# Rows for the convolution's layer norm and for later token rates: sent through DRAM in place of PE transposes

## The chip, the cores and the metric

The kernel runs on one core of a Trainium2 chip. The metric is the device time of one execution in microseconds, of which three were measured: 1282.7, 1285.05 and 1284.26 us, with a median of 1284.26 us. A profile of one further execution shows what each engine did: PE (matrix products and transposes, with its weight loads listed as PEld), DVE, ACT and POOL (element-wise work), and SP, which issues most of the transfers.

## The reference

One layer of a hybrid encoder runs over 2048 tokens of 1024 channels, with 16 learned tokens ahead of them. A projection feeds two groups: a gated depthwise convolution with a layer norm over channels, and a stick-breaking attention with 8 heads of 64 channels. Both are concatenated, projected again, normalised and added to the input.

```
u = rms_norm(h, pre_g)
proj = u @ w_in                      # 3584 columns: glu_a, glu_b, conv_gate, q, k, v, sb_gate
c = glu_a * sigmoid(glu_b)
c = causal_depthwise_conv(c, conv_w, conv_b)          # width 31
c = silu(layer_norm(c, conv_ln_g, conv_ln_b))         # mean and variance over 512 channels
c = (c @ w_pw2 + b_pw2) * silu(conv_gate)
s = stick_breaking_attention(q, k, v) * silu(sb_gate)
return h + rms_norm(concat([c, s]) @ w_out, post_g)
```

## The kernel before

Tokens are worked in four chunks of 512 (`TC`), c = 0 to 3. Activations lie turned: channels on the 128 partitions, tokens along the free axis, so a quantity that belongs to a token (a mean, a rate) has to stand as a row of 512 numbers that is the same on all partitions. Every float32 product is made of three passes with split high and low parts, and PE carries all of them.

A Python-side scheduler writes the program. It keeps a model clock (`Clock`, `Engine`), runs three streams of pieces against each other in `merge` (attention as `main`, projections, norm and output products as `fill`, and `extra`), and emits work noted with `when` as soon as the model says that its inputs are there. A piece that PE takes waits until the model has its inputs ready for `slack` (1.0 us). Any operation added or removed therefore shifts the order of everything emitted after it. Each engine then executes its own list strictly in order, and SP too: a transfer whose wait is not met holds all transfers behind it.

The part around the change is `conv_norm(c, accs)`. When the four convolution sums `accs[j]` of a chunk (128 channels x 512 tokens each) are there, PE turns them in four blocks of 128 tokens into a PSUM bank `T` (of which there are four), and DVE takes mean and variance per token (`bn_stats`, `bn_aggr`), which gives a column of 128 numbers. `rstd_of` makes the rate on POOL. Then the columns are made into rows twice, first the means and then the rates: four PE transposes of a broadcast column against the identity fill one bank `T`, and DVE applies the row to the four sums (`apply`, subtraction for i = 0, product with the gain for i = 1). `swish` follows, then `conv_parts` splits the result and `conv_out` multiplies it, much later in the program.

`spread_later(c)` does the same for the norm ahead of the input projection of chunks 1 to 3: four transposes of a column of `later` give the row of token rates, which ACT copies to the tile `row` for c > 1, and DVE multiplies it into the input tiles `xs` (`times_rate`, `scale`).

The lines that make a row of means or rates before:

```
rows[i] = PT("T", [P, TC])
for tb in range(NTB):
    pe.transpose(
        rows[i][:, tb * P : (tb + 1) * P], cols[tb].to_broadcast([P, P]), ident
    )
for j in range(NJ):
    when(
        lambda j=j, i=i: apply(j, i), [rows[i], accs[j]], [accs[j]]
    )
```

Of the kernel before, what the change touches and what calls it, by code (L numbers as in the profile page):

```python
# [11 lines left out]
F32 = mybir.dt.float32  # L12
F32R = mybir.dt.float32r
BF16 = mybir.dt.bfloat16
AF = mybir.ActivationFunctionType
ALU = mybir.AluOpType
# [3 lines left out]
P = 128  # L20
# [3 lines left out]
NM = 16  # L24
TC = 512
NCH = SEQ // TC
NTB = TC // P
CC = 512
NJ = CC // P
# [15 lines left out]
LAGS, LEAD = 1.5, 0.2  # L45
TAP, APART_TAP = 0.67, 1.25
EARLY = 6
LAG = 3

WINDOW = 10.0  # L50
# [226 lines left out]
def trunk(ctx: ExitStack, tc: tile.TileContext, x, xturn, xlater, meta, cpack, post_g, wpack, out):  # L277
    nc = tc.nc
# [15 lines left out]
    def when(what, ins, outs=(), engine=None, date=0.0, tag=None, late=0.0):  # L294
        soon.append(Later(clock, what, ins, outs, engine, date, tag, late))

    pe = Engine(clock, nc.tensor, pe_cost, 0.15, run)
    dve = Engine(clock, nc.vector, dve_cost, 0.04, run)
    act = Engine(clock, nc.scalar, act_cost, 0.04, run)
    pool = Engine(clock, nc.gpsimd, pool_cost, 0.04, run)  # L300
    sp = Engine(clock, nc.sync, sp_cost, 0.0, run)
# [9 lines left out]
    dr = ctx.enter_context(tc.tile_pool(name="dr", bufs=1, space=DRAM))  # L311
# [14 lines left out]
    def T(tag, shape, bufs, dt=F32):  # L326
        room(tag, bufs)
        t = sb.tile(shape, dt, tag=tag, name=tag, bufs=bufs)
        clock.take(tag, bufs, t.name)
        return t  # L330

    def PT(tag, shape):
        bufs = BANKS[tag]
        room(tag, bufs)
        t = ps.tile(shape, F32, tag=tag, name=tag, bufs=bufs)
        clock.take(tag, bufs, t.name)
        return t
# [3 lines left out]
    def need(*aps, tag=None, given=None, evs=0, n=1):  # L341

        def at():
            if given and not given():
                return 1e6
            t = max([clock.at(a) for a in aps] + [0.0])
            if tag:
                t = max(t, clock.next_free(tag, n))  # L350
            if evs:

                t = max(t, clock.next_free("ev", evs) - 1.0)
            return t + slack[0]

        return at


    ident = const.tile([P, P], F32, name="ident")
# [8 lines left out]
    lng = cp[:, o + NJ : o + 2 * NJ]  # L368
# [16 lines left out]
    row = const.tile([P, NM + TC], F32, name="row")  # L385
# [24 lines left out]
    vscr = dr.tile([NJ, NM + SEQ, 2 * P], F32, name="vscr")  # L410
    sscr = dr.tile([NCH, NJ, P, TC], F32, name="sscr")
    gscr = dr.tile([NCH, NJ, P, TC], F32, name="gscr")

    u_now = []
    xs = {}
# [20 lines left out]
    def tap_apart():  # L436
        tap(taps_apart)
# [11 lines left out]
    def rstd_of(acc, n, eps, rows=P, cols=1):  # L449
        v = T("st1", [P, cols], 4)  # L450
        pool.tensor_scalar(v[:rows], acc[:rows], 1.0 / n, eps, op0=ALU.mult, op1=ALU.add)
        r = T("st2", [P, cols], 8)
        pool.tensor_tensor(
            r[:rows], v[:rows], nhalf[:rows].to_broadcast([rows, cols]), op=ALU.pow
        )
        return r
# [93 lines left out]
    for turn, (w, n0, cols, ka, kb) in specs():  # L550
        step_k = 4 * P // cols
        for k0 in range(ka, kb, step_k):
            key = w, n0, cols, k0
            n = (min(k0 + step_k, kb) - k0) * cols
# [257 lines left out]
        renewed(c)  # L812

    def spread_later(c):
        pt = PT("av" if c == 1 else "T", [P, TC])
        for tb in range(NTB):
            n = (c - 1) * NTB + tb
            pe.transpose(
                pt[:, tb * P : (tb + 1) * P], later[:, n : n + 1].to_broadcast([P, P]), ident
            )  # L820
        keep["row", c] = pt
        if c > 1:
            act.activation(row[:, NM:], pt, AF.Copy)
            keep["row", c] = row[:, NM:]
        for k in range(KD):
            if (c, k) in xs:
                times_rate(c, k)

    later = T("sq2", [P, 4 * NTB], 1)
# [224 lines left out]
    def meta_v(h):  # L1054
        e, j = h % 2, h // 2
        force(f"v{j}")
        for g in range(3):
# [4 lines left out]
            )  # L1062
        if h >= EARLY:
            sp.dma_start(
# [17 lines left out]
    keep = {("z", -1): True}  # L1082
# [17 lines left out]
    def conv_apart(c, j):  # L1100
# [15 lines left out]
            pool.tensor_tensor(acc, acc, this, op=ALU.add)  # L1116
        accs[c][j] = acc

    def conv_norm(c, accs):
        def summed():  # L1120
            if len(accs) == NJ:
                return pe.now
            return max(dve.now, pool.now, pe.now) + 2.0 if taps or taps_apart else 1e6

        yield summed
        while taps:
            tap()
        while taps_apart:
            tap_apart()


        rows = {}
        rates = [None] * NTB

        def rate(tb, mv):
            rates[tb] = rstd_of(mv[:, 1:2], 1, 1e-5)

        means = []
        for tb in range(NTB):
            yield need(*(accs[j][:, tb * P : (tb + 1) * P] for j in range(NJ)), tag="T")  # L1140
            pt = PT("T", [P, CC])
            for j in range(NJ):
                pe.transpose(
                    pt[:, j * P : (j + 1) * P], accs[j][:, tb * P : (tb + 1) * P], ident
                )
            st = T("bst", [P, 6], 3)
            dve.bn_stats(st, pt)
            mv = T("bmv", [P, 2], 5)
            dve.bn_aggr(mv, st)
            means.append(mv)  # L1150
            when(lambda tb=tb, mv=mv: rate(tb, mv), [mv])
        done = []

        def apply(j, i):
            if i:
                dve.scalar_tensor_tensor(
                    accs[j], accs[j], lng[:, j : j + 1], rows[i], op0=ALU.mult, op1=ALU.mult
                )
            else:
                dve.tensor_tensor(accs[j], accs[j], rows[i], op=ALU.subtract)  # L1160
            done.append((j, i))

        for i in range(2):
            if i:
                yield need(given=lambda: None not in rates and len(done) == NJ)
            cols = rates if i else [mv[:, 0:1] for mv in means]
            yield need(*cols, tag="T")
            rows[i] = PT("T", [P, TC])
            for tb in range(NTB):
                pe.transpose(  # L1170
                    rows[i][:, tb * P : (tb + 1) * P], cols[tb].to_broadcast([P, P]), ident
                )
            for j in range(NJ):
                when(
                    lambda j=j, i=i: apply(j, i), [rows[i], accs[j]], [accs[j]]
                )
        yield need(given=lambda: len(done) == 2 * NJ)
        def swish(j):
            b, y, sg = lnb[:, j : j + 1], accs[j], PT("T", [P, TC])
            act.activation(sg, y, AF.Sigmoid, bias=b)  # L1180
            when(
                lambda: dve.scalar_tensor_tensor(y, y, b, sg, op0=ALU.add, op1=ALU.mult),
                [y, sg], [y],
            )

        for j in range(NJ):
            when(
                lambda j=j: swish(j), [accs[j]], [accs[j]], date=pe.now + 1.5 * j, tag="T"
            )
        keep["normed", c] = True  # L1190
# [73 lines left out]
    def attention(c, mixs):  # L1264
# [41 lines left out]
        def scan(r, u, zs, zr):  # L1306
# [18 lines left out]
            prev[r] = u["a"][r] = pr  # L1325
            if kc == 0 and c == NCH - 1 and h >= EARLY:
                bm = keep["bm"][:, h - EARLY, r, h]
                zm = sgm[:, r, h, 0:NM]
# [611 lines left out]
    accs = [{} for _ in range(NCH)]  # L1940
# [141 lines left out]
```

## Time and profile before

| what | value |
|---|---|
| median of three runs | 1284.26 us |
| the profiled execution's own time | 1282.96 us |
| its span, first to last instruction | 1281.2 us |
| busy PE / DVE / ACT / POOL | 1270.7 / 1009.5 / 790.0 / 681.0 us |
| granted PE clock | 0.999 |
| HBM traffic | 218.95 MB read, 66.98 MB written |

Busy time is the time in which an engine had at least one instruction under way. A matmul's duration runs from its start to a modelled end, and several overlap, so what one takes of PE's time is read from the distance between starts. "Idle before" is the time an engine stood still ahead of a group, with the engine or transfer whose signal ended it. The 1.76 us between span and time lie outside the first and last instruction.

### The profile page before, as it was taken

The page shows a single profiled execution, that of the slowest core. Times are in us where ns is not written, and L with a number is a line of the kernel's source. Part 1 is how long each engine was busy: PE and PEld are TensorE (multiplying, and loading weights), DVE is VectorE, ACT ScalarE, POOL GpSimd, SP SyncE. Part 2 cuts the span into 40 slices and gives each one's busy share as a digit, 9 for nine tenths or more (in the row PEclk, how much of TensorE's full clock was granted, in tenths as well). Part 3 has the DMA queues.
Part 4 walks back from the last instruction along what each step waited for, and adds up shares of the span by engine and source line. Part 5 has one row for each costly group of instructions (what it writes and reads, how often), then busy time and mean ns, then how long its engine had stood idle before and what let it go on. Part 6 is the DMA issues. An engine that isn't in the chain of part 4 may idle for free.

```text
span 1281.2 us, 22398 instructions
## 1 busy us (share of the span) xinstructions
PE 1270.7 (99%) x7463; PEld 1104.3 (86%) x7463; DVE 1009.5 (79%) x1434; ACT 790.0 (62%) x1696; POOL 681.0 (53%) x805
## 2 busy tenths in 40 slices
PE   9999999999999999999999999999999999999997
PEld 8998888888899888888889988888888899888897
DVE  5999998898987488984567587985548888899974
ACT  6544456445456464777655546789877766656553
POOL 2555569867687430677872231388788522232402
PEclk9999999999999999999999999999999999999999
DMA  6688876687988885676966695657668555576745
GB/s 245 214 275 266 268 252 220 208 262 244 288 274 270 292 294 178 209 234 211 295 198 212 178 339 176 179 180 230 201 223 256 150 152 185 169 250 216 222 150 183
DMA packets 175876, 289.79 MB, mean 226 GB/s; under 512 B 21120, under 2 KB 72512, under 8 KB 175760
## 3 DMA queue, kind: packets, MB, share of 16 engines
q1 hardware_dynamic: 164528, 250.87, 63.0%
q0 software_dynamic: 11232, 37.49, 7.8%
q8 instruction: 59, 0.97, 0.3%
q14 instruction: 57, 0.47, 0.1%
HBM read 218.95 MB, written 66.98 MB: 223 GB/s over the span
## 4 chain that ended last, share of the span: by engine, by line
PE 95%; DMA 2%; DVE 1%; POOL 1%; issue 0%; ACT 0%; SPq 0%; DVEq 0%; POOLq 0%; ACTq 0%
PE mm L228 63%; PE T L228 22%; PE av L228 10%; DMA tok<-x 1%; DMA wr<-wpack 0%; DVE ul L228 0%; PE cv L228 0%; DMA wr<-wscr 0%; DMA pr<-xturn 0%; DVE tok L228 0%; POOL st L228 0%; ACT ev L228 0%; DVE bst L228 0%; DVE T L228 0%; SPq L228 0%
## 5 line engine op out<-in xcount | busy, mean ns | idle before, releaser
L228 PE MATMUL mm<-uh,w 128*128 128x512 f32 (+1 forms) x1936 | 562.3, 376 | 0.0
L228 PEld LDWEIGHTS mm<-uh,w 128*128 128x128 f32 x1936 | 336.6, 188 | 50.9 <-ACT uh L228 0.3
L228 PE MATMUL mm<-ul,w 128*128 128x512 f32 (+1 forms) x968 | 358.2, 371 | 0.1
L228 DVE TENSOR_TENSOR_SCAN pr<-T,pr,zcol 128x512 f32<-128x512 f32 (+1 forms) x224 | 268.6, 1200 | 47.7 <-ACT T L228 37.7
L228 DVE TENSOR_TENSOR al<-T,ah 128x512 fp32r<-128x512 f32 (+1 forms) x320 | 191.6, 600 | 97.3 <-ACT ah L228 95.2
L228 DVE SCALAR_TENSOR_TENSOR cv<-ct,cp,cv 128x512 f32<-128x512 f32 x319 | 239.1, 750 | 6.8
L228 ACT ACTIVATE ah<-T 128x512 fp32r<-128x512 f32 (+1 forms) x320 | 169.3, 530 | 108.5 <-PE T L228 106.1
L228 POOL TENSOR_TENSOR acc<-acc,pd 128x512 f32<-128x512 f32 x150 | 193.6, 1290 | 59.3 <-ACT pd L228 52.1
L228 PEld LDWEIGHTS mm<-ul,w 128*128 128x128 f32 x968 | 181.3, 188 | 33.8 <-DVE ul L228 0.5
L228 POOL TENSOR_TENSOR w<-wr,w 128x512 fp32r<-128x512 f32 x130 | 169.9, 1309 | 66.8 <-ACT w L228 58.6
L228 ACT ACTIVATE T<-T 128x512 f32<-128x512 f32 (+5 forms) x352 | 169.7, 489 | 51.4 <-PE T L228 45.7
L228 ACT ACTIVATE w<-wr 128x512 fp32r<-128x512 f32 x220 | 137.9, 628 | 85.2 <-PE mm L228 45.1
L228 PE MATMUL T<-kk,q 128*128 128x512 f32 (+4 forms) x704 | 190.4, 365 | 0.0
L228 PE MATMUL T<-ident,pr 128*128 128x128 f32 x1088 | 171.1, 272 | 0.0
L228 PEld LDWEIGHTS T<-ident,pr 128*128 128x128 f32 x1088 | 134.2, 140 | 29.3 <-DVE al L228 0.2
L228 PEld LDWEIGHTS T<-kk,q 128*128 128x128 f32 x704 | 113.4, 189 | 14.4 <-DVE pr L228 0.7
L228 PE MATMUL av<-ah,vk 128*128 128x512 f32 (+1 forms) x320 | 117.7, 368 | 0.0
L228 PE MATMUL av<-al,vk 128*128 128x512 f32 (+1 forms) x320 | 116.9, 365 | 0.0
L228 DVE TENSOR_TENSOR_SCAN pr<-T,tri 128x128 f32<-128x128 f32 (+3 forms) x128 | 87.6, 688 | 33.0 <-ACT T L228 30.6
L228 ACT ACTIVATE pd<-ct,cp 128x512 f32<-128x512 f32 x150 | 105.6, 715 | 0.9 <-POOL acc L228 0.8
L228 POOL COPY cm<-pr 128x1 f32<-128x1 f32 x120 | 24.3, 203 | 124.3 <-DVE pr L228 117.9
L228 POOL TENSOR_TENSOR ev<-ev 64x512 f32<-64x512 f32 (+2 forms) x46 | 55.6, 1208 | 56.6 <-ACT ev L228 38.3
(202 smaller groups left out, 1570.7 us busy)
## 6 DMA issues: line engine op xcount, KB each, us to landing
wr<-wpack SPq DMA_DIRECT2D x220, 256.0 KB, 3.9
w<-wscr SPq DMA_DIRECT2D x70, 512.0 KB, 4.6
vk<-vscr SPq DMA_DIRECT2D x80, 256.0 KB, 3.5
w<-lscr SPq DMA_DIRECT2D x80, 256.0 KB, 2.7
kk<-kscr SPq DMA_DIRECT2D x72, 256.0 KB, 4.2
q<-qscr SPq DMA_DIRECT2D x64, 256.0 KB, 5.4
wscr<-w POOLq DMA_DIRECT2D x28, 512.0 KB, 4.8
lscr<-w POOLq DMA_DIRECT2D x40, 256.0 KB, 3.8
```

The lines of the kernel that those rows point to most:

```text
L228: return call(out, *args, **kw)
```

## The change

For chunks 1 to 3, the means and rates of the convolution norm no longer pass PE. A transfer on SP writes the column of 128 x 4 numbers to a small DRAM tile `nscr` as 512 consecutive numbers (`spread_out`), and a second one reads them back to all 128 partitions as a tile `nrow` in SBUF, 128 x 512 (`load`). It is noted for 6 us (`SPREAD`) after the first. There is one `nrow` buffer, so the rates' load waits until the means have been subtracted. Chunk 0 keeps its PE transposes. Token rates of chunks 2 and 3 go the same way, straight into `row`. The four mean and variance columns now lie in one tile `bmv`, and `rstd_of` runs once over four columns rather than four times over one. The room set aside for POOL's transfer descriptors is halved.

```
+    nscr = dr.tile([NCH, 3, 1, TC], F32, name="nscr")
...
     def spread_later(c):
+        if c > 1:
+            n = (c - 1) * NTB
+            date = spread_out(c, 2, later[:, n : n + NTB]) + SPREAD
+            when(lambda: row_later(c), [], date=date)
+            return
...
+    def row_later(c):
+        keep["row", c] = row[:, NM:]
+        sp.dma_start(row[:, NM:], nscr[c, 2].to_broadcast([P, TC]))
+        times_rates(c)
...
+    def spread_out(c, i, col):
+
+        sp.dma_start(nscr[c, i, 0].rearrange("(t p) -> p t", p=P), col)
+        return pe.now
...
+        mvs = T("bmv", [P, NTB, 2], 2)
+        sent, done = {}, []
+
+        def send(i, col):
+            sent[i] = spread_out(c, i, col) if c else col
+
+        def load(i):
+            t = T("nrow", [P, TC], 1)
+            sp.dma_start(t, nscr[c, i].to_broadcast([P, TC]))
+            put_in(i, t)
...
+        when(lambda: send(0, mvs[:, :, 0]), [mvs])
+        when(lambda: later_on(rstd_of(mvs[:, :, 1], 1, 1e-5, cols=NTB)), [mvs])
...
+        for i in range(2):
+            yield need(given=lambda: i in sent and len(done) == i * NJ)
+            if c:
+                when(lambda i=i: load(i), [], date=max(pe.now, sent[i] + SPREAD))
             else:
...
-    nc = _bacc.Bacc("TRN2", target_bir_lowering=False, num_devices=1, dynamic_dma_scratch_size=4096)
+    nc = _bacc.Bacc("TRN2", target_bir_lowering=False, num_devices=1, dynamic_dma_scratch_size=2048)
```

On PE, behind the turn of chunk 1's convolution sums, these rows stood before (`T<-ident,bmv` makes the row of means, `T<-ident,st` that of rates, `mm` rows are output products, `av` and `T<-kk` attention):

```order
L228 MATMUL av<-al,vk 128x512
L228 MATMUL T<-ident,bmv 128x128 x4
L228 MATMUL T<-ident,pr 128x128 x2
L228 MATMUL mm<-w,mixs 128x256 x12
L228 MATMUL T<-kk,q_4270 128x272 x2
L228 MATMUL av<-ah,vk 128x512
L228 MATMUL av<-al,vk 128x512
L228 MATMUL T<-ident,st_4677 128x128
L228 MATMUL T<-ident,st_4701 128x128
L228 MATMUL T<-ident,st_4720 128x128
L228 MATMUL T<-ident,st_4724 128x128
L228 MATMUL mm<-w,mixs 128x256 x12
```

The same place on PE now:

```order
L229 MATMUL av<-al,vk 128x512
L229 MATMUL mm<-w,mixs 128x256 x12
L229 MATMUL T<-ident,pr 128x128 x2
L229 MATMUL T<-kk,q_4256 128x272 x2
L229 MATMUL mm<-w,mixs 128x256 x12
L229 MATMUL av<-ah,vk 128x512
L229 MATMUL av<-al,vk 128x512
L229 MATMUL mm<-w,mixc 128x256 x12
```

Eight transposes are gone here, the rest stands in a slightly other order; in all PE has 7431 matmuls instead of 7463, with 12 fewer on `bmv`, 12 fewer on `st` and 8 fewer on the token rates `sq`, and no other kind changed in number.

On DVE, behind chunk 1's `BN_AGGR` (the mean and variance), this stood before; `acc<-acc,T` subtracts the means and `acc<-acc,cp,T` multiplies by rates and gain, while `al` and `pr` are attention:

```order
L228 SCALAR_TENSOR_TENSOR pr<-T,pr,zcol 128x512
L228 TENSOR_TENSOR acc<-acc,T 128x512 x4
L228 TENSOR_TENSOR al<-T,ah 128x256
L228 SCALAR_TENSOR_TENSOR pr<-T,tri 128x256
L228 SCALAR_TENSOR_TENSOR acc<-acc,cp,T 128x512 x4
L228 TENSOR_TENSOR al<-T,ah 128x128
```

DVE's list now, from the sixth row behind that `pr` on:

```order
L229 SCALAR_TENSOR_TENSOR pr<-T,tri 128x264
L229 SCALAR_TENSOR_TENSOR pr<-T,pr,zcol 128x248
L229 TENSOR_TENSOR acc<-acc,nrow 128x512 x4
L229 TENSOR_TENSOR al<-T,ah 128x512
L229 SCALAR_TENSOR_TENSOR pr<-T,tri 128x128
L229 SCALAR_TENSOR_TENSOR pr<-T,pr,zcol 128x512
L229 TENSOR_TENSOR al<-T,ah 128x512
L229 SCALAR_TENSOR_TENSOR acc<-acc,cp,nrow 128x512 x4
L229 TENSOR_TENSOR al<-T,ah 128x512
```

The subtraction stands seven attention rows further back than it did, and the product with the rates four rows behind the subtraction; both now read `nrow`.

On SP, the new transfers of chunk 1 stand so, between loads of weights (`wr`), keys, values and queries (`kk`, `vk`, `q`):

```order
L229 DMA nscr<-bmv 128x4x1
L229 DMA wr<-wpack 128x512 x2
L229 DMA nscr<-st_4696 128x4x1
L229 DMA vk<-vscr 128x4x128
L229 DMA kk<-kscr 128x512
L229 DMA q_4756<-qscr 64x2x512 x2
L229 DMA nrow<-nscr 128x512
L229 DMA wr<-wpack 128x512
L229 DMA nrow<-nscr 128x512
L229 DMA wr<-wpack 128x512
L229 DMA tok<-xlater 128x1024 x2
L229 DMA nscr<-sq_104 128x4x1
```

Five transfers were put in here, four of the norm and the write of chunk 2's token rates; the loads around them keep their order.

More of the change, by code (lines that the diff above doesn't have):

```diff
@@ L47 @@
 EARLY = 6
+SPREAD = 6.0
 LAG = 3
@@ L821, in spread_later, with times_rates @@
         keep["row", c] = pt
-        if c > 1:
-            act.activation(row[:, NM:], pt, AF.Copy)
-            keep["row", c] = row[:, NM:]
+        times_rates(c)
+    def row_later(c):
+        keep["row", c] = row[:, NM:]
+        sp.dma_start(row[:, NM:], nscr[c, 2].to_broadcast([P, TC]))
+        times_rates(c)
+    def times_rates(c):
         for k in range(KD):
@@ L1129, in conv_norm, with turn, put_in, apply @@
             tap_apart()
[L1132 to L1138, printed above, removed]
+        mvs = T("bmv", [P, NTB, 2], 2)
[6 more added lines that the diff above has]
+            put_in(i, t)
+        def turn(i):
+            t = PT("T", [P, TC])
+            for tb in range(NTB):
+                pe.transpose(
+                    t[:, tb * P : (tb + 1) * P],
+                    sent[i][:, tb : tb + 1].to_broadcast([P, P]), ident,
+                )
+            put_in(i, t)
+        def put_in(i, t):
+            for j in range(NJ):
+                when(lambda j=j: apply(j, i, t), [t, accs[j]], [accs[j]])
+        def apply(j, i, t):
+            if i:
+                dve.scalar_tensor_tensor(
+                    accs[j], accs[j], lng[:, j : j + 1], t, op0=ALU.mult, op1=ALU.mult
+                )
+            else:
+                dve.tensor_tensor(accs[j], accs[j], t, op=ALU.subtract)
+            done.append((j, i))
         for tb in range(NTB):
@@ L1147, in conv_norm, with later_on @@
             dve.bn_stats(st, pt)
[L1148 to L1158, printed above, removed]
-            else:
[L1160 to L1176, printed above, removed]
+            dve.bn_aggr(mvs[:, tb], st)
+        when(lambda: send(0, mvs[:, :, 0]), [mvs])
+        when(lambda: later_on(rstd_of(mvs[:, :, 1], 1, 1e-5, cols=NTB)), [mvs])
+        def later_on(r):
+            when(lambda: send(1, r), [r])
+        for i in range(2):
+            yield need(given=lambda: i in sent and len(done) == i * NJ)
+            if c:
+                when(lambda i=i: load(i), [], date=max(pe.now, sent[i] + SPREAD))
+            else:
+                yield need(sent[i], tag="T")
+                turn(i)
+            yield need(given=lambda: len(done) == (i + 1) * NJ)
         yield need(given=lambda: len(done) == 2 * NJ)
```

## The prediction

> **What bounds the kernel now.** The page's first part and its chain of waits come first, then the view of what PE waited for, then two of the 32 us windows.
>
> ```profile
> span 1281.2 us, 22398 instructions
> PE 1270.7 (99%) x7463; PEld 1104.3 (86%) x7463; DVE 1009.5 (79%) x1434; ACT 790.0 (62%) x1696; POOL 681.0 (53%) x805
> PE 95%; DMA 2%; DVE 1%; POOL 1%; issue 0%; ACT 0%; SPq 0%; DVEq 0%; POOLq 0%; ACTq 0%
> ...
> PE T L228 <- POOL ident masks.py:199: 1.7, 1, 1.7
> PE T L228 <- DVE ul L228: 1.3, 2, 0.7
> PE av L228 <- POOL rate L228: 0.6, 1, 0.6
> PE mm L228 <- POOL w L228: 0.2, 1, 0.2
> ...
> 384.00:416.00 32.00, 31.83 (x257) 30.91 (x256) 24.11 (x31) 20.39 (x54) 25.53 (x28) 1.00 0.83 272
> 1248.00:1280.00 32.00, 26.74 (x196) 25.03 (x194) 15.83 (x32) 11.04 (x29) 7.22 (x8) 0.98 0.55 186
> ```
>
> PE is busy 1270.7 of 1281.2 us and carries 95% of the chain that ends last. It waited 3.8 us in all (1.7 + 1.3 + 0.6 + 0.2), of which only the last 0.2 us lies behind chunk 0's first projections, in the window 384 to 416, where chunk 1's norm runs. The rest of its idle time is the tail (26.74 busy in the last window), which the change doesn't touch. So every microsecond of PE work that goes shortens the kernel by as much, unless a new wait takes its place; and no engine's busy time but PE's is near the span.
>
> **What goes: 32 transposes.** Their rows among the groups, and a stretch of PE's timeline in chunk 3:
>
> ```profile
> L228 PE MATMUL T<-ident,bmv 128*128 128x128 f32 x16 | 2.4, 272 | 0.0
> L228 PE MATMUL T<-ident,sq 128*128 128x128 f32 x8 | 1.2, 272 | 0.0
> ...
> 1060.38 0.60 PE L228 MATMUL T<-ident,bmv 128*128 128x128 f32 x4
> 1060.81 0.60 PE L228 MATMUL T<-ident,pr 128*128 128x128 f32 x4
> 1061.17 1.65 PE L228 MATMUL mm<-wr,mixs 128*128 128x256 f32 x12
> 1062.66 0.64 PE L228 MATMUL T<-kk,q 128*128 128x264 f32 x4
> ...
> 1063.60 1.57 PE L228 MATMUL mm<-wr,mixs 128*128 128x256 f32 x12
> 1065.01 0.60 PE L228 MATMUL T<-ident,pr 128*128 128x128 f32 x4
> ```
>
> A transpose lasts 272 ns but they overlap, so its price is the distance between starts. Four of `bmv` hold PE from 1060.38 to 1060.81, 0.43 us. The four of `pr` behind them take 0.36 us (to 1061.17), but then twelve products take 1.49 us (to 1062.66) where twelve of the same kind, not behind a transpose, take 1.41 us (1063.60 to 1065.01): the missing 0.08 us is paid there. So a set of four costs 0.43 to 0.44 us wherever it stands. Chunks 1 to 3 lose two sets each and chunks 2 and 3 one more each for the token rates: 8 x 0.435 = **3.5 us**. Chunk 0 keeps its eight. The order of the changed program confirms 32 matmuls fewer and no other kind changed in number, so that the change doesn't do what it says is excluded.
>
> The Trainium skill, page "TensorE: Matmul & The Clock Gate", section "Part 4: PE-mode transpose", gives about 275 ns for one such transpose in a kernel's context. The trace agrees as to duration (272) and not as to the time PE loses; the third rival below takes that duration for the price.
>
> **What comes: eight column writes and eight row loads.** Six of each belong to the norm, two to the token rates; a write has 512 pieces of 4 bytes, a load 256 KB. No transfer of the trace has 4-byte pieces. Landing times by the nearest rows:
>
> ```profile
> vk<-vscr SPq DMA_DIRECT2D x80, 256.0 KB, 3.5
> w<-lscr SPq DMA_DIRECT2D x80, 256.0 KB, 2.7
> kk<-kscr SPq DMA_DIRECT2D x72, 256.0 KB, 4.2
> tok<-xlater SPq DMA_DIRECT2D x12, 512.0 KB, 6.4
> ev<-x SPq DMA_DIRECT2D x24, 256.0 KB, 6.1
> pgs<-post_g SPq DMA_DIRECT2D x1, 512.0 KB, 5.4
> uh<-gscr SPq DMA_DIRECT2D x2, 256.0 KB, 6.7
> kk<-kscr SPq DMA_DIRECT2D x24, 8.0 KB, 3.7
> ```
>
> The write: `vk` has as many pieces (128 x 4 rows of 512 bytes) and lands in 3.5 us; `kk` of 8 KB has 128 pieces of 64 bytes and lands in 3.7. I take 3.6 us, between 2.7 and 6.7 us, the ends of the table. The load is noted 6 us behind the write, so it finds the column there unless the write is near its upper end. The page "DMA: Bandwidth & Descriptors" of the Trainium skill, section "Rules for kernel authors", says that a non-contiguous last dimension costs one descriptor per element, which speaks against this write; no run here shows yet what 512 such elements cost, and by the row of `vk` 512 pieces are within the 6 us.
>
> The row's load reads one DRAM row for all partitions, as `pgs` does (5.4 us for twice the bytes). I take 4.2 us, the row of `kk`, and 2.7 to 6.7 us as bounds.
>
> What hides this: nothing on PE reads `nrow` or `row`. Their only reader is DVE, and the norm's result is first multiplied (`conv_out`) long after the turn of the sums. In chunk 1:
>
> ```profile
> 376.43 1.91 PE L228 MATMUL T<-ident,acc 128*128 128x128 f32 x16
> ...
> 395.63 0.72 DVE L228 SCALAR_TENSOR_TENSOR acc<-acc,cp,T 128x512 f32<-128x512 f32 x1
> ...
> 456.92 1.64 PE L228 MATMUL mm<-mixs,w 128*128 128x512 f32 x6
> ```
>
> That is 80 us, of which the norm and its swish needed 20 (the last `acc<-acc,cp,T` ends at 396.35). Four transfers in a row, twice 3.6 + 4.2, lengthen it by some 16 us; chunks 2 and 3 have more attention in between. A later norm is therefore free. What can cost is only the order: DVE stands still at the first `acc<-acc,nrow` if the row hasn't landed, with `al` and `pr` of attention queued behind it, and SP stands still at a load that waits, with `vk`, `kk` and `w` behind it.
>
> For DVE, the trace has rows of the same sort, loads that DVE waits for at places set by the same model clock:
>
> ```profile
> L228 DVE SCALAR_TENSOR_TENSOR tok<-tok,st,ev 128x512 f32<-128x512 f32 x24 | 19.9, 830 | 3.3 <-DMA ev<-x 3.3
> L228 DVE TENSOR_TENSOR tok<-tok,row 128x512 f32<-128x512 f32 x16 | 14.3, 927 | 0.2 <-DMA tok<-xlater 0.2
> L228 DVE TENSOR_TENSOR acc<-acc,T 128x512 f32<-128x512 f32 x16 | 9.9, 679 | 0.3 <-PE T L228 0.3
> L228 DVE SCALAR_TENSOR_TENSOR acc<-acc,cp,T 128x512 f32<-128x512 f32 x32 | 22.4, 738 | 0.1
> L228 DVE SCALAR_TENSOR_TENSOR ul<-tok,cp,uh 128x512 fp32r<-128x512 f32 x24 | 21.4, 923 | 0.0
> ...
> 410.30 2.60 DVE L228 TENSOR_TENSOR tok<-tok,row 128x512 f32<-128x512 f32 x1
> 414.00 0.69 DVE L228 TENSOR_TENSOR al<-T,ah 128x512 fp32r<-128x512 f32 x1 [1.10 <-ACT ah L228]
> ```
>
> Forty instructions waited 3.5 us in all for `ev` and `tok`, 0.09 us each, and PE's list of waits has a single DVE entry, `ul`, in chunk 0's first projections. Eight new rows at the same rate per row wait 0.7 us; at the rate of `ev` alone (3 stops in 24, 1.1 us each) one stop of 1.1 us. The second price is that `apply` now reads two SBUF tiles where one operand lay in PSUM: `tok<-tok,row` takes 927 ns in the mean against 679 for `acc<-acc,T`, and `ul<-tok,cp,uh` 923 against 738 for `acc<-acc,cp,T`. Twelve of each: 12 x 0.25 + 12 x 0.185 = 5.2 us more on DVE, in six groups of four with at most about 1 us each; at the least nothing, as the commonest duration of `tok<-tok,row` is that of the others. That PE takes such a delay without a wait is shown at 410.30: an operation 1.9 us too long there is followed by 1.1 us in which DVE waits for ACT, not PE for DVE. I put both at **0** on PE, and at 3 us at the other end (each of six groups late by 1.5 us, of which the 1.0 us that PE's pieces are held back absorbs two thirds).
>
> The one tight place is chunk 1's second row. Its load waits on SP until the four subtractions are done, and on DVE's list only `al`, two scans and `al` stand between subtraction and product: 3.0 us of DVE work (0.67 + 0.42 + 1.28 + 0.67 by rows of the same forms) against 4.2 us of landing. If nothing else slowed DVE it would stand 1.2 us; at 6.7 us, 3.7 us. Chunks 2 and 3 have seven rows between.
>
> ```profile
> 707.77 0.42 DVE L228 TENSOR_TENSOR_SCAN pr<-T,tri 128x128 f32<-128x128 f32 x1 [0.85 <-ACT T L228]
> 708.30 1.28 DVE L228 TENSOR_TENSOR_SCAN pr<-T,pr,zcol 128x512 f32<-128x512 f32 x1
> 709.50 0.67 DVE L228 TENSOR_TENSOR al<-T,ah 128x512 fp32r<-128x512 f32 x1
> ...
> L228 POOL TENSOR_TENSOR st<-st,nhalf 128x1 f32<-128x1 f32 (+1 forms) x19 | 12.0, 634 | 1.6
> L228 POOL TENSOR_SCALAR st<-bmv 128x1 f32<-128x1 f32 x16 | 3.0, 187 | 12.6 <-DVE bmv L228 11.7
> ```
>
>
> Small items: POOL makes each chunk's rates in two instructions rather than eight (4 x (0.63 + 0.19) = 3.3 us before, at least half of it gone), around the 0.2 us that PE waited for POOL's `w`: up to 0.2 us gained, counted at 0. ACT's two copies into `row` go, beside other work. Halving POOL's descriptor room: POOL issues some 130 transfers, one per 10 us, and none of its kinds lands in over 5.5 us by the table of transfers, so few are ever open; 0, and at the other end one such landing where several come together. The 2 MB of row loads add under 1% to 219 MB read, and PE's waits name no transfer: 0.
>
> **Sum.** 1282.96 - 3.5 + 0 = 1279.5 us for the profiled execution. That execution lies 1.3 us under the median of 1284.26, so against the median 1284.26 - 3.5 = **1280.8 us**, 0.27% faster.
>
> **Rivals.** *The gain is partly given back* (late rows and slower `apply` reach PE). For it: eight new ordered waits on DVE and SP, and a changed order everywhere behind 380 us. Against it: the rows at 410.30 and PE's list of waits. A give-back of 1.5 us gives 1282.3, within 0.2% of before.
>
> *The second row of each norm becomes the wait* (slower). SP may issue it only when the subtractions are done, into the single `nrow`; DVE then stands at the product with attention behind it, and PE runs dry of `al`. At 3.7 us in each of three chunks this is 11.1 us, 1284.26 - 3.5 + 11.1 = 1291.9. It decides from 3.5 / 3 = 1.2 us of PE time per chunk on. Against it: two chunks have seven DVE rows in between, and PE's pieces wait 1.0 us by design.
>
> *A transpose costs its full duration.* Were 272 ns the price, 32 of them would be 8.7 us and the time 1275.6. Against it: the starts above, 0.43 us for four. The section on the PE-mode transpose named above would have it so.
>
> **Chances.** Forecast (1279 to 1281.7) 0.60; partly given back 0.24; second row becomes the wait 0.12; full duration 0.04. A measurement of this kernel tells about 0.2% (2.6 us) from no change, so faster means under 1281.7 and slower over 1286.8. The forecast lies 0.9 us inside that bound, and a small part of the first rival's share falls on the faster side: faster 0.63, within 0.2% 0.25, slower 0.12. The range leaves out the two extreme rivals (0.16): from 1278.8, the forecast with 0.2 us of POOL's wait gone and a spread of the runs of 1.8 us, to 1285.0, the forecast with 3 us on DVE and 1.2 us of spread.
>
> **What would show it.** Right: 7431 matmuls, PE's busy time near 1267, no `bmv`, `st` or `sq` transposes behind chunk 0, and no DVE or DMA entry over 0.5 us among PE's waits behind 65 us. Wrong: a line for DVE waiting on `nrow` of over 1.5 us per row with PE idle behind it; `nscr` landing later than 6 us; SP's waits for `nscr` with `kk` or `w` late behind them; or POOL's transfer issues idle for want of room. If PE's busy time falls by 3.5 us and the time doesn't, a wait took its place; if by clearly more, the slots were misread.

## The result and the profile after

| | before | after |
|---|---|---|
| median (runs) | 1284.65 us (4) | 1318.22 us (4) |
| ratio | | 1.0269, interval 1.0242 to 1.0297 |
| span of the profiled execution | 1281.2 us | 1315.7 us |
| PE busy / matmuls | 1270.7 us / 7463 | 1277.9 us / 7431 |
| granted PE clock | 0.999 | 0.991 |

The change costs 2.7%: the medians lie 33.6 us apart, the spans of the profiled executions 34.5 us, which is also what the ratio gives; 1280.8 us was forecast. The engines' line of the page and the chain of waits of the changed kernel:

```profile
PE 1277.9 (97%) x7431; PEld 1107.1 (84%) x7431; DVE 1010.0 (77%) x1434; ACT 788.8 (60%) x1694; POOL 674.8 (51%) x781
...
PE 84%; DMA 8%; DVE 4%; issue 2%; POOL 1%; ACT 1%; SPq 0%; POOLq 0%; DVEq 0%; ACTq 0%
```

32 matmuls are gone, and yet PE is busy 7.2 us longer and carries 84% of the chain where it carried 95%. Transfers, 2% before, have 8%. What PE waited for says which (us in total, times, longest):

```profile
PE T L229 <- DMA kk<-kscr: 10.9, 4, 7.9
PE mm L229 <- DMA w<-wscr: 9.8, 4, 5.5
```

Keys (`kk`) and weights (`w`) belong to no line of the change. They come late. The table of transfers (count, KB each, median us from issue to landing) and, as its last line, the landing of all transfers that write or read `nscr`, as far as the trace dates them (seven writes and six loads):

```profile
nscr<-bmv SPq DMA_DIRECT2D x3, 2.0 KB, 10.4
nscr<-st SPq DMA_DIRECT2D x3, 2.0 KB, 10.3
nscr<-sq SPq DMA_DIRECT2D x2, 2.0 KB, 11.8
nrow<-nscr SPq DMA_DIRECT2D x6, 256.0 KB, 4.3
row<-nscr SPq DMA_DIRECT2D x2, 256.0 KB, 6.7
...
DMA to landing us min/median/max: 4.1/10.2/23.0
```

A write of 2 KB lands after 10 to 12 us by these medians; the seven that are dated take 9.2 to 23.0 us. The loads' medians are near what was foreseen, but one load took 10.4 us, and the first, issued at 393.73 and not dated, let DVE go on only at 412.54. Chunk 1's place on SP, from the timeline (start and duration in us):

```profile
380.24 0.38 SPq L229 DMA_DIRECT2D nscr<-bmv  x1
380.71 1.35 SPq L229 DMA_DIRECT2D wr<-wpack  x2
382.15 0.95 SPq L229 DMA_DIRECT2D nscr<-st  x1
383.39 0.46 SPq L229 DMA_DIRECT2D vk<-vscr  x1
383.91 0.64 SPq L229 DMA_DIRECT2D kk<-kscr  x1
384.60 9.00 SPq L229 DMA_DIRECT2D q<-qscr  x2
393.73 0.52 SPq L229 DMA_DIRECT2D nrow<-nscr  x1
```

Keys and queries were issued 1.8 and 2.5 us behind the second write, so no wait of SP held them back; but the two `q` loads took 9.00 us to issue (1.41 at the same place of chunk 2), and but for one stretch (392 to 396) little moved until 404. In 4 us windows (length, busy time of PE, PEld, DVE, ACT and POOL, granted clock, DMA share, GB/s):

```profile
384.00:388.00 4.00, 4.00 (x34) 3.91 (x33) 1.11 (x2) 2.74 (x9) 3.20 (x5) 1.00 0.92 31
388.00:392.00 4.00, 3.09 (x25) 2.96 (x24) 0.00 (x0) 0.01 (x1) 1.29 (x1) 1.00 0.75 23
392.00:396.00 4.00, 3.50 (x29) 3.42 (x29) 1.83 (x3) 2.98 (x8) 1.71 (x2) 1.00 1.87 220
396.00:400.00 4.00, 3.77 (x33) 3.62 (x32) 1.55 (x3) 1.88 (x8) 3.35 (x5) 1.00 0.52 15
400.00:404.00 4.00, 0.00 (x0) 0.00 (x0) 0.00 (x0) 0.00 (x0) 1.83 (x2) 0.80 0.71 93
404.00:408.00 4.00, 0.31 (x1) 0.34 (x2) 0.00 (x0) 0.73 (x2) 0.03 (x1) 0.50 1.01 302
408.00:412.00 4.00, 4.00 (x18) 3.81 (x18) 0.00 (x0) 1.41 (x4) 1.83 (x2) 0.50 1.04 415
```

The last two columns are the reading: at a DMA share of 0.92 and 0.75 the engines deliver 31 and 23 GB/s, about a tenth of what they deliver from 404 on. (The share adds up the time that packets take, so a packet that is held counts too, and the sum can pass 1.) PE then has no keys; the load issued at 383.91 frees it at 407.69:

```profile
407.69 1.41 PE L229 MATMUL T<-kk,q 128*128 128x512 f32 x3 [7.91 <-DMA kk<-kscr]
408.89 2.76 PE L229 MATMUL mm<-w,mixs 128*128 128x256 f32 x12
...
412.54 2.50 DVE L229 TENSOR_TENSOR acc<-acc,nrow 128x512 f32<-128x512 f32 x4 [14.74 <-DMA nrow<-nscr]
413.10 1.57 PE L229 MATMUL mm<-w,mixs 128*128 128x256 f32 x12
```

PE stood still for 7.91 us, and twelve products behind the stop take 2.76 us where twelve of the same kind take 1.57 at 413.10: the granted clock is 0.50. DVE stood 14.74 us at the subtraction, with attention behind it.

The loss in the 32 us windows:

```profile
384.00:416.00 32.00, 22.68 (x164) 21.86 (x162) 7.92 (x13) 11.65 (x35) 13.24 (x15) 0.84 0.91 159
416.00:448.00 32.00, 27.23 (x191) 24.76 (x191) 17.88 (x26) 17.49 (x46) 17.14 (x21) 1.00 1.00 265
704.00:736.00 32.00, 24.94 (x182) 23.64 (x181) 15.33 (x21) 11.07 (x33) 4.26 (x7) 0.89 0.51 148
736.00:768.00 32.00, 30.43 (x216) 28.09 (x216) 23.05 (x31) 18.91 (x44) 10.58 (x14) 1.00 0.70 210
1088.00:1120.00 32.00, 29.70 (x208) 27.41 (x207) 24.58 (x33) 17.51 (x43) 5.89 (x7) 0.95 0.73 155
```

PE is idle 9.3, 4.8, 7.1, 1.6 and 2.3 us in them, 25 us together, all at the three norms and the token rates behind them. Most of the rest is work at the lower clock: PE's busy time rose by 7.2 us although the transposes left it.

### The profile page after: what moved, and what is told of

Its sections match the earlier page's. It is cut to its first block, busy times and chain, and to the rows that moved or that the text cites. A ratio compares the mean times of both kernels' runs of the same rounds, so it can differ in the third digit from the quotient of the medians.

```text
span 1315.7 us, 22325 instructions
## 1 busy us (share of the span) xinstructions
PE 1277.9 (97%) x7431; PEld 1107.1 (84%) x7431; DVE 1010.0 (77%) x1434; ACT 788.8 (60%) x1694; POOL 674.8 (51%) x781
## 2 busy tenths in 40 slices
DMA packets 181252, 291.91 MB, mean 222 GB/s; under 512 B 25472, under 2 KB 76864, under 8 KB 181136
## 4 chain that ended last, share of the span: by engine, by line
PE 84%; DMA 8%; DVE 4%; issue 2%; POOL 1%; ACT 1%; SPq 0%; POOLq 0%; DVEq 0%; ACTq 0%
PE mm L229 55%; PE T L229 19%; PE av L229 9%; DMA w<-wscr 2%; DMA wr<-wpack 2%; DMA wscr<-w 2%; DVE pr L229 1%; DMA kk<-kscr 1%; POOL w L229 1%; DVE ul L229 1%; DMA tok<-x 1%; DVE tok L229 0%; PE cv L229 0%; ACT ev L229 0%; DMA pr<-xturn 0%
## 5 line engine op out<-in xcount | busy, mean ns | idle before, releaser
L229 PE MATMUL mm<-w,mixc 128*128 128x256 f32 x600 | 82.8, 286 | 9.6 <-DMA w<-wscr 8.6
```

The costliest lines, as they stand in the source:

```text
L229: return call(out, *args, **kw)
```

## The experiments

Theory A: a column write of 512 pieces of 4 bytes is slow, and holds the transfers beside it. Rivals: the waits for the rows, the changed order (with `apply` on two SBUF tiles), the loads, and POOL's halved descriptor room (D in the expectations). Within A, A1 says that pieces sharing lines of DRAM are slow, A2 that short pieces are slow by themselves. Except where the text says so, every engine's list stands as in the changed kernel, apart from the transfers of the edit. Where a constant is written or loaded, the rows are not the means and rates, and the result is not the layer's. The kernel before, run beside them, took 1283.06 to 1283.62 us (medians).

**Long pieces.** The write takes a constant, in 4 pieces of 512 B.

```
-        sp.dma_start(nscr[c, i, 0].rearrange("(t p) -> p t", p=P), col)
+        sp.dma_start(nscr[c, i, 0].rearrange("(t p) -> t p", p=P), ident[:NTB])
```

> The changed kernel, but each of its eight writes to nscr sends 2 KB of a constant tile in 4 pieces of 512 bytes in place of a column in 512 pieces of 4 bytes; the rows are then not the means and rates. The order of PE and DVE is that of the changed kernel, SP still waits for each write before its load, and DVE for each load. Theory A (the 4-byte pieces hold the transfers): the write lands in about 3.5 us instead of 10, no 8 us wait of PE for kk or w is left, and the time is 1284.5 - 3.5 = 1281 us. Rival B (the chain of waits, SP behind the write and DVE behind the row, at any size of the pieces): over 1300 us. Rival C (the new order itself runs PE dry): 1318 us as the changed kernel.

Measured: 1286.14 us, ratio 1.0021 (1.0012 to 1.0029). The trace dates none of these writes; the load behind the third one was issued 5.9 us after it. So 32 of the 34.5 us hang on the form of the write (that a constant is sent instead of the column doesn't explain it: own neighbours, below, sends one too). But no gain from the transposes shows.

**Half the descriptor room, in the kernel before.**

```
-dynamic_dma_scratch_size=4096
+dynamic_dma_scratch_size=2048
```

> The kernel before with POOL's descriptor room halved and nothing else. Theory A and rivals B and C: within 0.2% of before, 1284.5 us. Rival D (POOL's transfers wait for room): slower by 10 to 34 us, with POOL idle ahead of its transfers.

Measured: 1283.53 us, ratio 1.0000 (0.9991 to 1.0009). In this kernel the room costs nothing.

**Rows from elsewhere.** The writes stay; the loads read a DRAM row written once.

```
-            sp.dma_start(t, nscr[c, i].to_broadcast([P, TC]))
+            sp.dma_start(t, nfix.to_broadcast([P, TC]))
```

> The changed kernel with its 4-byte writes, but all rows are loaded from a DRAM row that is written once at the start, so no load waits for a write; the rows are constants. Theory A: the transfers queued behind the writes (kk, w, and the rows themselves) still land late, PE still waits 5 us and more for them, and most of the loss stays: 1300 to 1318 us. Rival B: with SP's wait for the write gone, 1281 to 1286 us.

Measured: 1309.44 us, ratio 1.0203 (1.0184 to 1.0222), two runs. No load needs a write's data now, and three quarters of the loss remain. PE's waits in this kernel:

```profile
PE T L229 <- DMA kk<-kscr: 9.5, 4, 4.1
PE mm L229 <- DMA w<-wscr: 5.1, 2, 4.1
```

For the greater part it is the writes' being under way that costs, not the need for what they wrote. Two waits are not quite gone: SP stood 5.5 us in chunk 1 until the first write had landed (28.5 us in all in the changed kernel, by its list of waits), but the keys had been issued ahead of that stop; and DVE still waited 16.6 us for late rows (21.4 in the changed kernel).

**Own lines.** As the last, with each 4-byte piece 512 B from the next, in a DRAM tile `far`.

```
+    far = dr.tile([NCH, 3, TC, P], F32, name="far")
...
+        sp.dma_start(far[c, i].rearrange("(t p) e -> p t e", p=P)[:, :, 0:1], col.unsqueeze(2))
```

> As the kernel whose rows come from elsewhere, but each 4-byte piece goes to a place 512 bytes from the next, so that no two pieces share 512 bytes of DRAM. If the pieces are slow because 16 engines change the same few lines (A1), the write lands in 3.5 to 5 us and the time is near 1281 us. If each 4-byte piece is slow by itself (A2), the write lands in 10 us as in the changed kernel and the time is as with rows from elsewhere.

Measured: 1286.92 us (one run). As many pieces of 4 bytes, and the loss is gone: what counts is where they lie. At this point the theory read: pieces that share a 512 B line of DRAM wait for one another.

**16-byte pieces.** Each partition's four numbers lie together, so a write has 128 pieces that touch.

```
-        sp.dma_start(nscr[c, i, 0].rearrange("(t p) -> p t", p=P), col)
+        sp.dma_start(nscr[c, i, 0].rearrange("(p t) -> p t", p=P), col)
```

> The changed kernel with the column written in another order: each partition's 4 numbers lie together in DRAM, so a write is 128 pieces of 16 B (32 to a 512 B line) in place of 512 pieces of 4 B (128 to a line); means and rates come in another order of tokens. If the cost of sharing a line goes by the number of pieces, a write that took 10 to 12 us takes a quarter of the excess over the 3.4 to 4.8 us of unshared pieces: 5 to 6 us landing, and the time is about 1290 to 1295 us. If it goes by bytes in a shared line or by the number of writes, it stays at 10 to 12 us and 1310 to 1318 us.

Measured: 1286.17 us (one run). Better than any expectation: nothing of the 30 us is left, though 32 pieces share a line. The shared-line theory is in doubt.

**64, 16 and 8 bytes apart.** As with own lines, the last size of `far` being 16, 4 and 2.

> The changed kernel with its 4-byte pieces written 64 B apart into another DRAM tile, 8 to a 512 B line, and rows loaded from a constant DRAM row (not the means and rates). Pieces 512 B apart landed in 3.4 to 4.8 us; pieces that touch in 10 to 12. If the cost is that of sharing 512 B, whatever the number of sharers: 10 us or more, 1305 to 1310 us as with touching pieces and a constant row. If it grows with the sharers of a line: 4 to 6 us, 1286 to 1290. If what counts is sharing 64 B or less: 3.4 to 4.8 us, about 1287.

> As the run with pieces 64 B apart, with 16 B from piece to piece: 32 to a 512 B line, 4 to 64 B. It has as many pieces to a line as the run with 16-byte pieces, but 512 in all. If the sharing of 512 B lines counts by their sharers: about a quarter of the touching pieces' excess in each line over four times the lines, 5 to 8 us landing, 1288 to 1298 us. If what counts is sharing of 64 B: 6 to 10 us, 1295 to 1306. If only pieces within 16 B of one another are slow: 3.4 to 4.8 us, about 1287.

> The changed kernel with its 4-byte pieces 8 B apart in another DRAM tile, and rows loaded from a constant DRAM row (not the means and rates). 16 B apart they landed in 4.5 to 6.7 us (1285), touching ones in 11 to 18 (1308). If the cost steps in where two pieces share 8 or 16 B: 8 to 12 us, 1295 to 1306 us. If only touching pieces are slow: 4 to 7 us, 1284 to 1288 us.

Measured: 1286.47, 1284.91 and 1287.16 us (one run each; kernels of this kind scatter between 1283 and 1289). None is slow. Sharing lines of 512 or 64 B, or 16 bytes, is not by itself the cause, and that theory fell. The packets and two of the windows of the kernel with 8 B from piece to piece:

```profile
DMA packets 181260, 291.91 MB, mean 227 GB/s; under 512 B 25476, under 2 KB 76872, under 8 KB 181144
...
384.00:388.00 4.00, 4.00 (x34) 3.91 (x33) 1.12 (x2) 2.67 (x9) 3.10 (x6) 1.00 0.84 192
388.00:392.00 4.00, 4.00 (x35) 3.97 (x34) 1.48 (x3) 2.58 (x6) 3.39 (x4) 1.00 1.04 289
```

There are 181260 packets, as many as in the changed kernel (its page has 181252), and 192 and 289 GB/s at the place where the changed kernel moved 31 and 23.

**Own neighbours.** 4-byte pieces that touch, but neighbours within 16 bytes come from one partition.

```
+        sp.dma_start(nscr[c, i, 0].rearrange("(p t) -> p t", p=P), ident[:, 0 : 2 * NTB : 2])
```

> The changed kernel with 4-byte pieces that touch in DRAM, as in the change, but with the four pieces of each 16 B from one partition (a constant read with a step of 8 B, so the rows are not the means and rates); in the change neighbours come from neighbouring partitions. If touching 4-byte pieces are slow whatever they come from: landing 10 us or more, 1305 to 1318 us. If they are slow since neighbours come from different partitions: 3 to 6 us, 1284 to 1288 us.

Measured: 1320.13 us (one run), as slow as the change. Its row among the transfers:

```profile
nscr<-ident SPq DMA_DIRECT2D x8, 2.0 KB, 13.0
```

Touching is enough, whichever partitions the neighbours come from. All the writes in one table:

| pieces of a write | landing, medians (us) | time (us) |
|---|---|---|
| 512 x 4 B touching, the change | 10.4 / 10.3 / 11.8 | 1318.22 |
| the same, constant rows loaded | 11.3 / 17.7 / 12.2 | 1309.44 |
| touching, neighbours from one partition | 13.0 | 1320.13, one run |
| 512 x 4 B, 8 B apart | 5.3 / 8.4 / 9.9 | 1287.16, one run |
| 16 B apart | 4.5 / 6.7 / 8.5 | 1284.91, one run |
| 64 B apart | 3.5 / 5.4 / 8.3 | 1286.47, one run |
| 512 B apart | 3.4 / 4.8 / 8.3 | 1286.92, one run |
| 128 x 16 B touching | 3.4 / 6.1 / 8.0 | 1286.17, one run |
| 4 x 512 B touching | not dated | 1286.14 |

(The three numbers are the writes of `bmv`, `st` and `sq`, each the median of the one to three that the trace dates; the single number of own neighbours is the median of three.) The step is between the third row and the fourth, in the time and in what the other transfers get; the landings overlap, since a write behind other work lands late in every form (`sq` up to 10.3 us with 8 B from piece to piece).

**No writes, and no transfers at all.** These ask where the 3.5 us of the transposes went. In the first, the rows are loaded from a constant; in the second, the loads are gone too, and `apply` reads a row in SBUF.

```
-        sp.dma_start(nscr[c, i, 0].rearrange("(t p) -> p t", p=P), col)
+        modelled(nscr[c, i, 0].rearrange("(t p) -> p t", p=P), col)
...
-            sp.dma_start(t, nscr[c, i].to_broadcast([P, TC]))
+            modelled(t, nscr[c, i].to_broadcast([P, TC]))
```

(These are the lines of the second; `modelled` moves the scheduler's clock and issues nothing. In it SP issues 970 transfers in place of 986, so 16 are gone, not the 18 of the expectation below.)

> The changed kernel without the writes to nscr; nrow and row are loaded from a DRAM row written once early (a constant, so the rows are not the means and rates). Theory A (transfers), if the writes are what is left: as the run without transfers, about 1280 us; if the loads are: as the run with long pieces, about 1286 us. Rival R (order and operands): 1286 us whichever transfers are there. The shared-lines theory wants PE's waits on kk and w below 2 us each here, since no write of short pieces is left.

> The changed kernel without any of its new transfers: no write to nscr and no load of nrow or row; the applies read a row that already lies in SBUF (the token rates of chunk 0), so the rows are not the means and rates. All engines' instructions stand in the changed kernel's order, only SP's list is 18 transfers shorter. It asks where the 3.5 us of removed transposes went in the run with long pieces, which came out 0.2% above the kernel before. Theory A (transfers): the remaining loads and writes, in order on SP, delay the loads of w and kk behind them; without them the transposes' 3.5 us show: 1280 us, ratio 0.997 to 0.998. Rival R (the new order, and applies that read two SBUF operands): nothing in it hangs on the transfers: 1286 us, ratio 1.001 to 1.003.

Measured: without writes 1285.56 us, ratio 1.0017 (1.0008 to 1.0025); without transfers 1282.26 us, ratio 0.9986 (0.9977 to 0.9995). The eight loads alone thus cost 0.0031 x 1284 = 4.0 us. Two windows show where, first of the kernel without writes, then of that without transfers:

```profile
384.00:416.00 32.00, 31.50 (x254) 30.49 (x253) 21.10 (x28) 19.53 (x52) 22.97 (x26) 1.00 0.83 289
672.00:704.00 32.00, 30.72 (x238) 29.07 (x237) 21.37 (x31) 14.83 (x39) 7.89 (x11) 1.00 0.66 207
```

```profile
384.00:416.00 32.00, 32.00 (x261) 31.32 (x260) 23.24 (x29) 19.70 (x52) 23.86 (x27) 1.00 0.84 282
672.00:704.00 32.00, 32.00 (x250) 30.61 (x249) 21.70 (x31) 15.76 (x42) 7.88 (x11) 1.00 0.63 204
```

PE loses 0.5 + 1.3 = 1.8 us there, and the two spans differ by 1.5 (1282.1 and 1280.6). PE's waits in the kernel without transfers, behind the first projections:

```profile
PE T L230 <- DMA kk<-kscr: 1.6, 2, 1.0
...
PE T L230 <- DVE al L230: 0.7, 1, 0.7
```

Neither is there before; the shifted order is the likely source, but that was not tested. The place in chunk 2, in 4 us windows of the kernel without writes:

```profile
694.00:698.00 4.00, 4.00 (x33) 3.91 (x32) 2.69 (x5) 2.47 (x8) 0.50 (x1) 1.00 1.02 265
698.00:702.00 4.00, 2.72 (x21) 2.28 (x20) 3.86 (x5) 1.34 (x4) 0.95 (x1) 1.00 1.02 363
```

The DMA engines are full (1.02) with keys, queries, weights and the 1 MB of the next chunk's tokens when the rows are fetched, and `w` comes 1.3 us late. The other 2 us or so show only in the medians over the runs; no view of the one profiled execution places them. The kernel with rows from elsewhere differs from the one without writes by the eight writes alone: they cost 0.0186 x 1284 = 23.9 us though no load needs them.

**One turn of the column.** PE turns the 128 x 4 column once, ACT copies it, and 4 pieces of 512 B are written; the whole layer is computed. The order shifts.

```
+        pe.transpose(pt[:NTB, :P], col, ident)
+        flat = T("ncol", [NTB, P], 1)
+        act.activation(flat, pt[:NTB, :P], AF.Copy)
+        sp.dma_start(nscr[c, i, 0].rearrange("(t p) -> t p", p=P), flat)
```

> Computes the whole layer, with the write in long pieces: PE turns the column of 128x4 numbers once (4x128 in PSUM, one transpose in place of four), ACT copies it to SBUF, and the write is 4 pieces of 512 B; the broadcast load stays. 24 transposes less than before (2.6 us of PE at 0.109) and 8 ACT copies more, of 4x128. Shared-lines theory: the write lands in 3 to 5 us, the 30 us of the change are gone, and the time is that of the run with long pieces plus about 1: 1283 to 1288 us, ratio 0.999 to 1.004. If the write of these columns were slow for another reason (data that come late, or the queue), it stays near 1310 to 1318 us.

Measured: 1293.39 us, ratio 1.0073 (1.0059 to 1.0087). The loss of the touching pieces is gone, as theory A has it, but 5 us above the expectation appear. PE waits 3.7 us once for DVE's `acc` in chunk 1, which it doesn't in the order of the change. That the order explains all of it was not shown.

**16-byte pieces put in order by DVE, and for the norm alone.** DVE reads `nrow` with a step of four numbers; in the second kernel the token rates go back to PE, which shifts the order.

```
+            put_in(i, t.rearrange("q (p t) -> q t p", p=P))
```

> Computes the whole layer. The column is written as 128 pieces of 16 B (each partition's four numbers together in DRAM), loaded as before, and DVE reads nrow and row with a step of four numbers, which puts the tokens back in order; every engine's list stands as in the changed kernel. Shared-lines theory: the writes land in 3 to 8 us as in the run with 16-byte pieces, PE waits under 2 us on kk and under 3 us on w, about 1286 us, ratio 1.001 to 1.003; the broadcast loads' 3 to 4 us stay in it. Rival: DVE's stepped reads are slow (twice the 0.69 us of an apply or more, 56 instructions, 20 to 40 us of DVE beside PE), which makes DVE late for attention at the norm: 1288 to 1300 us, with PE waiting on DVE.

> As the run with 16-byte pieces in order, but the token rates of chunks 2 and 3 are turned on PE and copied by ACT as in the kernel before: only the norm's means and rates go through DRAM. Two writes and two 256 KB loads less beside the 1 MB loads at the turn of a chunk, 8 transposes more (0.9 us). Theory that the loads cost by sharing full DMA engines (256 KB at the 370 GB/s of the kernel is 0.7 us each, behind which w comes late): 1284 to 1285.5 us, ratio 1.000 to 1.002. Rival R (order decides): no better than the run with both, 1286 us or above, since the order shifts too.

Measured: 1294.77 us, ratio 1.0084 (1.0070 to 1.0098), and 1298.91 us, ratio 1.0120 (1.0107 to 1.0134). The rival won in the first: stepped reads on DVE reach PE. The second can't tell what it was to tell, since it has them too.

**16-byte pieces put in order by PE.** The sums are turned with a step, so the column has the tokens in the order in which they lie in DRAM; DVE reads without a step; the whole layer is computed.

```
-                    pt[:, j * P : (j + 1) * P], accs[j][:, tb * P : (tb + 1) * P], ident
+                    pt[:, j * P : (j + 1) * P], accs[j].rearrange("q (p t) -> q t p", t=NTB)[:, tb], ident
```

> Computes the whole layer. The column is written as 128 pieces of 16 B and lies in DRAM in the tokens' own order, since PE turns the sums with a step (block tb takes tokens tb, tb+4, tb+8, ...; the stationary operand is read with a step of 16 B), and the rows of x behind the token rates are loaded in the same order; DVE reads nrow and row without a step, as in the change. Theory: with both costs gone (pieces that touch, stepped reads on DVE) it takes what the run with 16-byte pieces out of order took: 1284.5 to 1287.5 us, ratio 1.001 to 1.003, above the kernel without transfers by the loads. Rival: stepped weight loads are slow (48 of them, each up to 0.5 us more, or 24 us): 1290 us or more.

Measured: 1286.47 us, ratio 1.0024 (1.0012 to 1.0036), inside the expectation. DVE's rows (ns, minimum, median and maximum), first of the kernel with DVE's step, then of this one:

```profile
L229 DVE TENSOR_TENSOR acc<-acc,nrow x12: 1062/1099/2241, 394.7 to 1090.4; 128x512 f32<-128x512 f32 x12
L229 DVE SCALAR_TENSOR_TENSOR acc<-acc,cp,nrow x12: 1126/1148/2196, 405.7 to 1101.5; 128x512 f32<-128x512 f32 x12
L229 DVE TENSOR_TENSOR tok<-tok,row x16: 1033/1088/1471, 416.7 to 780.8; 128x512 f32<-128x512 f32 x16
```

```profile
L229 DVE TENSOR_TENSOR acc<-acc,nrow x12: 678/684/1776, 395.6 to 1081.0; 128x512 f32<-128x512 f32 x12
L229 DVE SCALAR_TENSOR_TENSOR acc<-acc,cp,nrow x12: 727/744/1787, 405.5 to 1090.1; 128x512 f32<-128x512 f32 x12
L229 DVE TENSOR_TENSOR tok<-tok,row x16: 658/678/929, 415.9 to 774.2; 128x512 f32<-128x512 f32 x16
```

Each stepped operation takes 0.40 to 0.42 us more, 40 of them 16.4 us; the two times differ by 8.3 us. About half of a delay on DVE came through to the end, with PE at 98 to 99%.

So no version that computes the layer is faster than the kernel before. The form of the write can be mended (1.0269 to 1.0024), the loads stay, and even without any transfer the change is worth 1.8 us (0.6 to 3.0).

## Why the prediction was wrong

**The failed step is the landing of the write**: "I take 3.6 us, between 2.7 and 6.7 us, the ends of the table". It is 10 to 12 us by the medians and 9.2 to 23.0 us singly, beyond the upper end, and worse, it is paid by others. The rows behind the price, `vk` with 512 pieces and the small `kk`, have pieces of 512 and 64 B; I took the count of pieces as what counts, and both are right as to count: 512 pieces of 4 B that do not touch land in 3.4 to 5.3 us at the first write of chunk 1, ahead of other work. What no row of before had is pieces of 4 B side by side.

**"What can cost is only the order"** missed the second half: transfers hold one another up. A transfer was priced by its own landing, and its reader asked; what else was in flight was not. The window quoted for chunk 1 had a DMA share of 0.83. The transfers of that share, PE's keys and weights, are what the writes held up: 23.9 us of the loss come without any load that needs a write. The loads added 4.0 us where I put "0".

**Term 1, the transposes (3.5 us).** Without any transfer the gain is 1.8 us, with an interval of 0.6 to 3.0 that leaves 3.5 out. In the profile of that kernel PE is busy 1268.2 us, 2.5 less than before and not 3.5, and there are 2.3 us of new PE waits behind the first projections (1.6 for `kk`, 0.7 for `al`). 3.5 - 2.3 = 1.2 lies inside the interval, so these waits could explain the smaller gain, but whether the slot of 0.435 us holds in full stays open. That PE gets no new waits from the changed program, even without transfers, was wrong.

**Rows awaited by DVE.** Named as a sign of error, and it came: 14.74 us in chunk 1, 21.4 us in all over five stops. It is an effect of the slow write; with no load that needs a write, 16.6 us of it and 1.0203 of 1.0269 remain. The sign named for SP came too: it stood 28.5 us for `nscr` (18.4 for `sq`, 10.1 for `bmv`).

**`apply` on two SBUF tiles.** Right: medians 686 and 744 ns, against 680 and 741 with a PSUM operand. The mean of 927 ns behind the other price came from a few long ones: `tok<-tok,row` has a median of 683 ns before, and a longest of 2601. But "I put both at 0 on PE" holds for such small delays only: 16.4 us of stepped reads cost 8.3.

**"A later norm is free."** Not refuted: in the mended kernels the norm still passes through its transfers, and PE doesn't wait for its result. **POOL's room at 0**: right, as tested in the kernel before.

**The rivals.** The slower one had the right sign with another mechanism: it put the wait at each norm's second row, and 19.4 of DVE's 21.4 us were at the subtractions, the first row. No rival had a transfer that delays transfers, and its price, 11 us, was a third of the loss.

**The sum as it stands**: -1.8 (transposes and order) + 4.0 (loads) + 0.0252 x 1284 = 32.4 (touching pieces, from 1.0269 against 1.0017) = 34.6 us. It closes by construction, since each term is the difference of two of the ratios. The last term is 23.9 us for writes that no load needs and 8.5 us for the loads' need of them; in it are, for the greater part, the 25 us of idle PE, and the work at half clock behind the stops.

## What to carry to other kernels

Price a new transfer by what it does to those in flight beside it: look at DMA share and GB/s of the very stretch, in windows of a few us, and doubt any price taken from rows with longer pieces. A column that must go to DRAM is better written in pieces of 16 B or more, or with gaps, which cost nothing that showed here; and its order was put right at less cost where PE reads the operand (1.0024) than by stepped reads on a DVE that feeds PE (1.0084). And when the engine that bounds is 99% busy, what a change removes from it is worth at most its slots, so bound the gain first: here 3.5 us, of which 1.8 were measured.

## What the runs showed of the hardware

**Touching 4-byte pieces.** 512 pieces of 4 B that lie side by side in DRAM land in 10 to 13 us (medians) and cost 24 to 32 us over eight writes; the same pieces 8 B apart, with as many packets, cost nothing that shows. Meanwhile other transfers crawl (31 and 23 GB/s in chunk 1; 104 and 102 GB/s from 1096 to 1104 in chunk 3), and not by keeping the DMA engines at work: in chunk 2, the two writes were issued at 702.86 and 704.28, and the windows behind them in the changed kernel read

```profile
704.00:708.00 4.00, 4.00 (x35) 3.91 (x34) 2.57 (x3) 1.96 (x7) 0.61 (x3) 1.00 0.08 1
708.00:712.00 4.00, 4.00 (x33) 3.83 (x33) 2.55 (x3) 2.10 (x6) 1.49 (x2) 1.00 0.00 0
```

The engines are idle, and both writes are still on their way: they land at 713.0 and 713.5. From the second write to 708.95 nothing else was issued, so idle engines are no loss by themselves; but a load of `w` issued then moves nothing before 713 either, and lands after 8.8 us (median 4.9). Between 706 and 713 the trace has no packet of any kind, so whatever holds the writes is not a packet that it shows. Nor is it settled whether the cause is two pieces within the same 8 B, the touching itself, or more pieces to a stretch (512 B hold 128 of them in the change, 64 with 8 B from piece to piece). Touching pieces of 16 B are quick, which speaks against touching by itself; pieces of 4 B that touch only across a bound of 8 B were not tried.

**The clock behind a stop.** After 7.91 us without work PE ran at 0.50 for over 4 us, twelve products taking 2.76 in place of 1.57 us; the granted clock was 0.80 over the window 400 to 404, so it fell while PE stood still. The Trainium skill, page "TensorE: Matmul & The Clock Gate", section "Why this matters for your kernels", says that a gap of over about 3 us sends the clock back to half; the trace agrees with that.

**Stepped operands.** A step of 16 B in one operand takes a DVE instruction on 512 columns from 0.684 to 1.099 us. The Trainium skill, page "Vector Engine (DVE) Microarchitecture Reference", section "5.2 Measured stream behaviour on trn2 (trn3 not measured)", has 1.73 against 1.054 ns per column where one source hops by 4 KiB at every element, by estimate 0.35 us more for 512 columns; the step here is 16 B, and the measured 0.41 is near. On PE the weight load of the sums with that step takes 209 in place of 141 ns (median), and the transposes 283 in place of 273, which did not show in the time beside the unstepped kernel with 16-byte pieces (1286.47 and 1286.17).
